# Thirteen pairs of up products a layer in place of twelve, and the block sums made kind by kind

## The chip, the cores and the metric

The kernel runs on one core of one Trainium2 chip. The time is the device time of one execution in microseconds (us); several runs are taken and their median is given. The core has five engines with queues of their own: TensorE (PE, matrix products), VectorE (DVE), ScalarE (ACT), GpSimd (POOL) and SyncE (SP, which issues the loads here). Products land in PSUM buffers, all else lies in SBUF.

## The reference

A trunk of two layers on x of 512 positions by 1024 features, float32. Each layer has a mixer (attention, a gated convolution and a recurrence, behind one input and one output projection), and then the part that matters here, a squared-ReLU MLP of 4096 hidden features:

```python
        x = x + mixed @ w_out[l]

        h = rms_norm(x, norm_mlp_g[l])
        x = x + jnp.square(jax.nn.relu(h @ w_mlp_up[l])) @ w_mlp_down[l]
    return rms_norm(x, final_norm_g)
```

## The kernel before

Everything is kept transposed: x is eight tiles `x[0..7]` of 128 features by 512 positions. Products are made nearly exact in float32 by splitting each operand into a rounded part (hi) and a rest (lo), and adding three products: hi·hi, hi·lo, lo·hi. So every weight block of 128x512 is loaded (`raw`, L339 or L1450), rounded by ScalarE (`whi`, L344; `shi_p`, L1455) and its rest taken by VectorE (`wlo`, L345; `slo_p`, L1456).

The MLP has 32 up groups of 128 hidden features. `up(i)` (L1405) makes one directly, a "single": 8 slices of the input, three matmuls of 512 columns each, 24 in all, through `mm3`. The first three singles are issued by TensorE within the end of the mixer. `two(i0, i1)` (L1443) makes two groups at once, a "pair": input, weights and output are cut in 2x2 blocks, and seven block products take the place of eight. A block product has 4 slices, three matmuls of 256 columns each; a pair has 7 × 12 = 84. Its seven products are p1, p5, p6, p2, p7, p3, p4 in that order, summed in three PSUM buffers `pa`, `pb`, `pc`. For them VectorE sums blocks of weights (`s1` to `s4`, L1461) and blocks of the input.

The sums of input blocks are the same for all pairs, and are made once a layer: `by_gain(j)` (L1420, ScalarE) writes `bn`, x with the norm's gain; `blocks(k)` (L1430) makes, for slice k, the four kinds of sums by VectorE subtractions of 128x256 (L1433 to L1436), ScalarE rounds them (`thi`), VectorE takes the rests (`tlo`, L1441). That is done for one k behind each of the singles 4 to 7.

Each up product goes through `square`: VectorE takes max(0, ·) times the norm's factor from PSUM (`r`, L1400), ScalarE squares it (`m`) and rounds it (`mh`), GpSimd takes the rest (`ml`, L1392). `mids` is the list of results, in ten buffers, and four of them make a "down group": `down(h, js)` (L1510) makes 8 tiles of 12 matmuls each, in two PSUM buffers in turn (tag "mm"), and VectorE adds each tile to x (`x<-dn`, L1516), which frees the buffer. The third tile waits for the first one's add.

The order in the MLP is: the singles; `down(0)`, all eight tiles; then the pairs, with half a down group (four tiles) behind a pair once `len(mids) >= 4 * h + 6`. With eight singles that holds after the first pair and after each one that follows, but for the last pairs of the last layer. Each engine runs its queue in order. That order is set at build time by a scheduler that places each instruction when it reckons its inputs and buffers to be there; so an instruction may stand earlier or later in its engine's queue than in the code.

`MID` (L184) is the order of the hidden features in mids, by which the host lays out the rows of the down weights.

Of the kernel before, what the change touches and what calls it, by code (L numbers as in the profile page):

```python
# [10 lines left out]
F32 = mybir.dt.float32  # L11
F32R = mybir.dt.float32r
# [4 lines left out]
ALU = mybir.AluOpType  # L17
# [6 lines left out]
P = 128  # L24
NK = D // P
# [150 lines left out]
         "wp/wlo 01201201201201202102102102102102102102102102102102102102102102102102102102 ")  # L176
NG = NG_IN + NG_OUT + NG_UP + NG_DN

N_ONE = 8

WHOLE = 5
PT = 1
N_TWO = (NG_UP - N_ONE) // 2
MID = tuple(range(N_ONE)) + tuple(N_ONE + i + N_TWO * j for i in range(N_TWO) for j in range(2))  # L184

# [83 lines left out]
def tile_trunk(ctx: ExitStack, tc: tile.TileContext, xT, wts, prm_d, cst_d, lora_d, gup_d, lam_d, fin_d, out):  # L269
    nc = tc.nc  # L270
    act, dve, pool = nc.scalar, nc.vector, nc.gpsimd
# [27 lines left out]
    def psum(tag, bufs, name):  # L299
        return ps.tile([P, 512], F32, tag=tag, bufs=bufs, name=name)  # L300
# [56 lines left out]
    def mm3(out_ps, w, acts, n=NK):  # L357
        for _ in mm3_steps(out_ps, w, acts, n):
            pass
# [12 lines left out]
    def norm_tile(j, key):  # L372

        if j == 0:
            acc = wp.tile([P, S], F32, tag="acc", bufs=1, name=f"acc{key}")
            nrm[key] = [acc]
            act.activation(acc, x[j], AF.Square)
        else:
            sq = wp.tile([P, S], F32, tag="sq", bufs=2, name=f"sq{key}_{j}")
            act.activation(sq, x[j], AF.Square)  # L380
            dve.tensor_tensor(nrm[key][0], nrm[key][0], sq, ALU.add)
# [187 lines left out]
    for l in range(L):  # L569
# [807 lines left out]
        with ExitStack() as mx:  # L1377
            fp = mx.enter_context(tc.tile_pool(name=f"fp{l}", bufs=1))
            spare[0] = fp
            RING = 10  # L1380
            H = S // 2
# [13 lines left out]
            def square(cs, name):  # L1395

                r = fp.tile([P, S], F32, tag="r", bufs=2, name=f"r{name}")
                for i, c in enumerate(cs):
                    q = slice(i * H, i * H + c.shape[1])
                    dve.scalar_tensor_tensor(r[:, q], c, 0.0, rs[:, q], ALU.max, ALU.mult)  # L1400
                m = fp.tile([P, S], F32, tag="m", bufs=3, name=f"m{name}")
                act.activation(m, r, AF.Square)
                kept(m)
# [9 lines left out]

            bn, th = {}, {}
            none = cp.tile([P, NB], F32, tag="rr", bufs=2, name=f"none{l}")[:, :1]
            dve.tensor_scalar(none, rs[:, :1], 0.0, None, ALU.is_lt)

            def by_gain(j):  # L1420

                if j == 0:
                    fp.tile([P, 8], F32, tag="pad0", name=f"pad0_{l}")
                bn[j] = fp.tile([P, 2, H], F32, tag="shi" if j < 4 else "slo", bufs=5, name=f"bn{l}_{j}")
                if j == 4:
                    fp.tile([P, 24], F32, tag="pad1", name=f"pad1_{l}")
                act.activation(bn[j].rearrange("p a s -> p (a s)"), x[j], AF.Identity, scale=pr[:, C_GMLP + j:C_GMLP + j + 1],
                               bias=none)

            def blocks(k):  # L1430
                b1, b2 = bn[k], bn[k + 4]
                t = [fp.tile([P, 2, H], F32, tag=f"s{2 * (k % 2) + i + 1}", name=f"t{l}_{k}_{i}") for i in range(2)]
                dve.tensor_tensor(t[0][:, 0], b1[:, 1], b1[:, 0], ALU.subtract)  # L1433
                dve.tensor_tensor(t[0][:, 1], b2[:, 1], t[0][:, 0], ALU.subtract)
                dve.tensor_tensor(t[1][:, 0], b2[:, 1], b1[:, 1], ALU.subtract)
                dve.tensor_tensor(t[1][:, 1], b2[:, 0], t[0][:, 1], ALU.subtract)  # L1436
                hi, lo = th[k] = [fp.tile([P, 4, H], F32R, tag=f"t{p}{k}", name=f"t{p}{l}_{k}") for p in ("hi", "lo")]
                for i in range(2):
                    u = slice(2 * i, 2 * i + 2)
                    act.copy(hi[:, u], t[i])  # L1440
                    dve.tensor_tensor(lo[:, u], t[i], hi[:, u].bitcast(F32), ALU.subtract)  # L1441

            def two(i0, i1):  # L1443

                n = f"{l}_{i0}"
                wg = wbase + NG_IN + NG_OUT

                def raw(i, a):
                    t = fp.tile([P, 4, P], F32, tag="sraw", bufs=6, name=f"raw{n}_{i}_{a}")
                    nc.sync.dma_start(t.rearrange("p k c -> p (k c)"), wts[wg + i, :, a * P:(a + 4) * P])  # L1450
                    return t

                def both(src, name):
                    hi, lo = [fp.tile([P, 4, P], F32R, tag=f"s{p}", bufs=5, name=f"s{p}{n}_{name}") for p in ("hi", "lo")]
                    act.copy(hi, src)  # L1455
                    dve.tensor_tensor(lo, src, hi.bitcast(F32), ALU.subtract)  # L1456
                    return hi, lo

                def sum_(name, a, b, op):
                    t = fp.tile([P, 4, P], F32, tag=name, name=f"{name}{n}")  # L1460
                    dve.tensor_tensor(t, a, b, op)  # L1461
                    return t

                def small(name):
                    return fp.tile([P, H], F32, tag=name, bufs=2, name=f"{name}{n}")

                def product(pt, w, moving, first=True):

                    whi, wlo = w
                    for k in range(4):  # L1470
                        ahi, alo = moving(k)
                        pe.matmul(pt, whi[:, k], ahi, start=(first and k == 0), stop=False, skip_group_check=True)
                        pe.matmul(pt, whi[:, k], alo, start=False, stop=False, skip_group_check=True)
                        pe.matmul(pt, wlo[:, k], ahi, start=False, stop=(k == 3), skip_group_check=True)

                blk = lambda d, q: lambda k: [p[:, q * H:(q + 1) * H] for p in acts[4 * d + k]]
                smm = lambda q: lambda k: [p[:, q] for p in th[k]]
                pa, pb = [psum("rp", 4, f"p{i}{n}")[:, :H] for i in "ab"]
                pc = psum("at", 2, f"pc{n}")[:, :H]
                c0 = fp.tile([P, S], F32, tag="c0", bufs=2, name=f"c0{n}")  # L1480
                w11 = raw(i0, 0)
                product(pa, both(w11, "p1"), blk(0, 0))
                p1 = small("p1")
                act.copy(p1, pa)
                w21 = raw(i1, 0)
                w22 = raw(i1, 4)
                s1 = sum_("s1", w21, w22, ALU.add)
                product(pb, both(s1, "p5"), smm(0))
                p5 = small("p5")
                dve.tensor_copy(p5, pb)  # L1490
                s2 = sum_("s2", s1, w11, ALU.subtract)
                product(pa, both(s2, "p6"), smm(1), False)
                u2 = small("u2")
                act.copy(u2, pa)
                w12 = raw(i0, 4)
                product(pc, both(w12, "p2"), blk(1, 0))
                dve.tensor_tensor(c0[:, :H], pc, p1, ALU.add)
                s3 = sum_("s3", w11, w21, ALU.subtract)
                product(pa, both(s3, "p7"), smm(2), False)
                c1 = small("c1")  # L1500
                act.copy(c1, pa)
                dve.tensor_tensor(c1, c1, p5, ALU.add)
                s4 = sum_("s4", w12, s2, ALU.subtract)
                product(pb, both(s4, "p3"), blk(1, 1), False)
                dve.tensor_tensor(c0[:, H:], pb, u2, ALU.add)
                square([c0], f"{n}_0")
                product(pa, both(w22, "p4"), smm(3), False)
                square([pa, c1], f"{n}_1")

            def down(h, js):  # L1510

                g, k0 = h // 2, 4 * (h % 2)
                for j in js:
                    pt = psum("mm", 2, f"dn{l}_{h}_{j}")
                    mm3(pt, weights(wbase + NG_IN + NG_OUT + NG_UP + 8 * g + j, k0, k0 + 4), mids[4 * h:4 * h + 4], 4)
                    dve.tensor_tensor(x[j], pt, x[j], ALU.add)  # L1516
                    if h == 2 * N_KG - 1 and j < NK - LATE:
                        norm_tile(j, f"m{l + 1}")


            for i in range(N_ONE):
                up(i)
                if i >= N_ONE - 4:
                    k = i - N_ONE + 4
                    by_gain(k)
                    by_gain(k + 4)
                    blocks(k)
            down(0, range(NK))
            h, half = 1, 0
            for p in range(N_TWO):  # L1530
                two(N_ONE + p, N_ONE + N_TWO + p)
                if len(mids) >= 4 * h + 6 and h < 2 * N_KG - 2 * (l == L - 1):
# [75 lines left out]
```

## Time and profile before

| | |
|---|---|
| runs | 1242.72, 1240.58, 1241.8 us; median 1241.8 |
| span of the profiled execution | 1241.5 us (no other time of it is given), granted clock 0.998 |
| busy: PE, DVE, ACT, POOL | 1230.0, 912.1, 675.0, 368.0 us |
| singles up_3 to up_7, layer 0 | 298.10 to 325.30 us |
| singles up_3 to up_7, layer 1 | 907.50 to 934.71 us |
| `down(0)`, layer 0 | 325.30 to 347.07 us |
| `down(0)`, layer 1 | 934.71 to 956.84 us |
| first pair, layer 0 | 347.07 to 357.07 us |
| last two pairs, layer 1 | 1166.11 to 1186.17 us |

Rows of the trace read: start, length (us), engine, line, operation, output<-inputs, shapes; in brackets the engine's idle time before it and what ended it. A row's length includes the time until its result is there, so that starts of neighbours (the pitch) tell what an engine spends on each. A row that is much longer than others of its shape was held up.

### The profile page before, as it was taken

How to read it: one execution, taken by the hardware profiler on the slowest of the kernel's cores; microseconds unless marked ns; L12 is line 12 of the kernel's file. 1: busy time of each engine (PE TensorE's matmuls, PEld its weight loads, DVE VectorE, ACT ScalarE, POOL GpSimd, SP SyncE). 2: the span in 40 equal slices, each digit the busy share in tenths (PEclk: the TensorE clock that was granted, in tenths of full speed). 3: DMA queues.
4: the chain of work that ended last, by engine and by line, in shares of the span. 5: the costliest groups of instructions: out<-in, count | busy, mean ns of one | idle time of the engine just before them, and what ended most of it. 6: DMA issues, size and time to landing. Idle time of an engine off the chain costs nothing.

```text
span 1241.5 us, 24974 instructions
## 1 busy us (share of the span) xinstructions
PE 1230.0 (99%) x9492; PEld 1055.0 (85%) x9492; DVE 912.1 (73%) x1776; ACT 675.0 (54%) x1410; POOL 368.0 (30%) x457
## 2 busy tenths in 40 slices
PE   9999999999999999999999999999999999999997
PEld 6888888888899998989887888888888999998987
DVE  6787888868767676765766777887687767676753
ACT  6785655548445454544464657464583445454542
POOL 1263637342311111111026355464231211111111
PEclk9999999999999999999999999999999999999999
DMA  6523324142433333321235244332433333333121
GB/s 216 163 87 99 105 96 111 53 153 85 136 102 98 107 94 106 99 85 44 69 106 164 79 118 119 89 83 73 158 102 120 102 102 98 107 94 107 55 68 68
DMA packets 84695, 127.90 MB, mean 103 GB/s; under 512 B 21472, under 2 KB 25568, under 8 KB 84576
## 3 DMA queue, kind: packets, MB, share of 16 engines
q1 hardware_dynamic: 83568, 125.64, 33.1%
q8 instruction: 74, 1.21, 0.4%
q10 hardware_dynamic: 1008, 0.68, 0.2%
q14 instruction: 45, 0.37, 0.1%
HBM read 117.11 MB, written 9.18 MB: 102 GB/s over the span
## 4 chain that ended last, share of the span: by engine, by line
PE 93%; ACT 2%; DVE 2%; DMA 1%; POOL 1%; issue 1%; ACTq 0%; POOLq 0%; DVEq 0%
PE dn L282 25%; PE pj L282 20%; PE pa L282 11%; PE po L282 8%; PE up L282 7%; PE pb L282 6%; PE dnF L282 4%; PE pc L282 3%; PE sc L282 1%; DMA raw<-wts 1%; PE ptt L287 1%; PE pg L282 1%; PE pyy L282 1%; PE pzw L282 1%; PE pst L282 1%
## 5 line engine op out<-in xcount | busy, mean ns | idle before, releaser
L1392 POOL TENSOR_TENSOR ml<-m,mh 128x512 fp32r<-128x512 f32 x64 | 108.9, 1716 | 481.0 <-ACT mh L1391 340.6
L344 ACT CAST whi<-raw 128x512 fp32r<-128x512 f32 x142 | 87.4, 619 | 162.4 <-PE dn L282 152.8
L282 PE MATMUL dn<-mh,whi 128*128 128x512 f32 x448 | 174.8, 390 | 0.1
L282 PE MATMUL dn<-ml,whi 128*128 128x512 f32 x448 | 174.6, 390 | 0.0
L282 PE MATMUL dn<-mh,wlo 128*128 128x512 f32 x448 | 174.5, 390 | 0.0
L683 POOL TENSOR_TENSOR wlo<-raw,whi 128x512 fp32r<-128x512 f32 x84 | 111.0, 1321 | 213.1 <-ACT whi L671 175.4
L282 PE MATMUL pj<-ahim,whi 128*128 128x512 f32 x392 | 156.7, 400 | 0.4 <-DVE vf L1278 0.4
L282 PE MATMUL pj<-ahim,wlo 128*128 128x512 f32 x392 | 156.4, 399 | 0.0
L282 PE MATMUL pj<-alom,whi 128*128 128x512 f32 x392 | 155.9, 398 | 0.0
L1516 DVE TENSOR_TENSOR x<-dn,x 128x512 f32<-128x512 f32 x112 | 77.3, 690 | 103.1 <-PE dn L282 103.1
L671 ACT CAST whi<-raw 128x512 fp32r<-128x512 f32 x142 | 87.6, 617 | 83.3 <-PE pj L282 25.1
L345 DVE TENSOR_TENSOR wlo<-raw,whi 128x512 fp32r<-128x512 f32 x142 | 115.0, 811 | 11.2 <-ACT whi L344 8.3
L282 PEld LDWEIGHTS dn<-mh,wlo 128*128 128x128 f32 x448 | 84.1, 188 | 17.8
L282 PEld LDWEIGHTS dn<-mh,whi 128*128 128x128 f32 x448 | 84.1, 188 | 17.5 <-issue 0.4
L282 PEld LDWEIGHTS dn<-ml,whi 128*128 128x128 f32 x448 | 84.1, 188 | 16.7
L1455 ACT CAST shi_p<-s 128x512 fp32r<-128x512 f32 x96 | 59.6, 621 | 70.1 <-PE pa L282 55.1
L282 PEld LDWEIGHTS pj<-ahim,whi 128*128 128x128 f32 x392 | 73.9, 188 | 14.1 <-issue 0.8
L282 PEld LDWEIGHTS pj<-alom,whi 128*128 128x128 f32 x392 | 73.9, 188 | 13.9 <-issue 0.5
L282 PEld LDWEIGHTS pj<-ahim,wlo 128*128 128x128 f32 x392 | 73.9, 188 | 13.8 <-issue 0.2
L1456 DVE TENSOR_TENSOR slo_p<-s,shi_p 128x512 fp32r<-128x512 f32 x96 | 67.9, 708 | 19.7 <-ACT shi_p L1455 17.2
L282 PE MATMUL pa<-tlo,shi_p 128*128 128x256 f32 x288 | 81.3, 282 | 0.0
L282 PE MATMUL pa<-thi,shi_p 128*128 128x256 f32 x288 | 81.2, 282 | 0.0
(414 smaller groups left out, 3208.1 us busy)
## 6 DMA issues: line engine op xcount, KB each, us to landing
raw<-wts SPq DMA_DIRECT2D x389, 256.0 KB, 2.7
qs<-dqhi SPq DMA_DIRECT2D x24, 128.0 KB, 3.7
ks<-dkhi SPq DMA_DIRECT2D x24, 128.0 KB, 3.7
x<-xT SPq DMA_DIRECT2D x8, 256.0 KB, 4.6
dqhi<-qhi SPq DMA_DIRECT2D x6, 256.0 KB, 3.4
dqlo<-qlo SPq DMA_DIRECT2D x6, 256.0 KB, 3.4
dkhi<-khi SPq DMA_DIRECT2D x6, 256.0 KB, 2.7
dklo<-klo SPq DMA_DIRECT2D x6, 256.0 KB, 3.5
```

Of the source, the lines that this page charges most:

```text
L282: ins = nc.tensor.matmul(*a, **k)
L287: ins = nc.tensor.transpose(*a, **k)
L344: act.copy(hi[:, :n], raw[:, :n])
L345: (pool if a and lean[0] else dve).tensor_tensor(lo[:, :n], raw[:, :n], hi[:, :n].bitcast(F32), ALU.subtract)
L671: yield act.copy(hi[:, k0:k1], raw[:, k0:k1])
L683: yield eng.tensor_tensor(lo[:, k0:k1], raw[:, k0:k1], hi[:, k0:k1].bitcast(F32), ALU.subtract)
L1392: pool.tensor_tensor(lo, m, hi.bitcast(F32), ALU.subtract)
L1455: act.copy(hi, src)
L1456: dve.tensor_tensor(lo, src, hi.bitcast(F32), ALU.subtract)
L1516: dve.tensor_tensor(x[j], pt, x[j], ALU.add)
```

## The change

`N_ONE` goes from 8 to 6: six singles and thirteen pairs a layer. `by_gain` of all eight tiles stands behind the singles and ahead of `down(0)`; `blocks` stands behind `down(0)` in the code and makes one kind q of sum for all slices, where it made all four kinds for one slice. The sums are written to the tiles `s3`, `s4` and `c0`, where they took `s1` to `s4`. The subtractions, casts and rests are as many as before, of the same shapes. `down(0)` stood ahead of the pairs before too; with six singles the condition for a half down holds only after the second pair, so that pairs one and two follow each other directly. A layer has two weight blocks of 128x512 (whi, wlo) less per single that goes, and one pair more of weight sums.

```diff
-N_ONE = 8
+N_ONE = 6
...
-            def blocks(k):
-                b1, b2 = bn[k], bn[k + 4]
-                t = [fp.tile([P, 2, H], F32, tag=f"s{2 * (k % 2) + i + 1}", name=f"t{l}_{k}_{i}") for i in range(2)]
-                dve.tensor_tensor(t[0][:, 0], b1[:, 1], b1[:, 0], ALU.subtract)
-                dve.tensor_tensor(t[0][:, 1], b2[:, 1], t[0][:, 0], ALU.subtract)
-                dve.tensor_tensor(t[1][:, 0], b2[:, 1], b1[:, 1], ALU.subtract)
-                dve.tensor_tensor(t[1][:, 1], b2[:, 0], t[0][:, 1], ALU.subtract)
-                hi, lo = th[k] = [fp.tile([P, 4, H], F32R, tag=f"t{p}{k}", name=f"t{p}{l}_{k}") for p in ("hi", "lo")]
+            def blocks(q):
+                hi, lo = th[q] = [fp.tile([P, 4, H], F32R, tag=f"t{p}{q}", name=f"t{p}{l}_{q}") for p in ("hi", "lo")]
                 for i in range(2):
                     u = slice(2 * i, 2 * i + 2)
-                    act.copy(hi[:, u], t[i])
-                    dve.tensor_tensor(lo[:, u], t[i], hi[:, u].bitcast(F32), ALU.subtract)
+                    t = fp.tile([P, 2, H], F32, tag="c0" if q == 1 else ("s3", "s4")[i], bufs=1 + (q == 1), name=f"t{l}_{q}_{i}")
+                    for k in (2 * i, 2 * i + 1):
+                        b1, b2, o = bn[k], bn[k + 4], t[:, k % 2]
+                        if q == 0:
+                            dve.tensor_tensor(o, b1[:, 1], b1[:, 0], ALU.subtract)
+                        elif q == 1:
+                            dve.tensor_tensor(o, b2[:, 1], tb[0, i][:, k % 2], ALU.subtract)
+                        elif q == 2:
+                            dve.tensor_tensor(o, b2[:, 1], b1[:, 1], ALU.subtract)
+                        else:
+                            dve.tensor_tensor(o, b2[:, 0], tb[1, i][:, k % 2], ALU.subtract)
+                    tb[q, i] = t
+                    act.copy(hi[:, u], t)
+                    dve.tensor_tensor(lo[:, u], t, hi[:, u].bitcast(F32), ALU.subtract)
...
-                smm = lambda q: lambda k: [p[:, q] for p in th[k]]
+                smm = lambda q: lambda k: [p[:, k] for p in th[q]]
...
             for i in range(N_ONE):
                 up(i)
-                if i >= N_ONE - 4:
-                    k = i - N_ONE + 4
-                    by_gain(k)
-                    by_gain(k + 4)
-                    blocks(k)
+            for j in range(NK):
+                by_gain(j)
             down(0, range(NK))
+            for q in range(4):
+                blocks(q)
```

Three places in the engines' queues show what the scheduler made of it. In all names the digit in front is the layer, the last number a buffer's.

The first is VectorE in layer 1, from the last single's r to the adds of the first tiles of `down(0)`. Before:

```order
L1400 SCALAR_TENSOR_TENSOR r1_7_11973<-up1_7_11936,rsf1_11639 128x512
L345 TENSOR_TENSOR wlo167_0_12061<-raw167_0_12058,whi167_0_12060 128x512
L1516 TENSOR_TENSOR x0_69<-dn1_0_0_11997,x0_69 128x512
L345 TENSOR_TENSOR wlo168_0_12081<-raw168_0_12078,whi168_0_12080 128x512
L1516 TENSOR_TENSOR x1_70<-dn1_0_1_12017,x1_70 128x512
L345 TENSOR_TENSOR wlo169_0_12101<-raw169_0_12098,whi169_0_12100 128x512
L1516 TENSOR_TENSOR x2_71<-dn1_0_2_12037,x2_71 128x512
```

The same place with the change:

```order
L1400 SCALAR_TENSOR_TENSOR r1_5_11903<-up1_5_11866,rsf1_11709 128x512
L345 TENSOR_TENSOR wlo167_0_11993<-raw167_0_11990,whi167_0_11992 128x512
L1447 TENSOR_TENSOR tlo1_3_12126<-t1_3_1_12132,thi1_3_12125 128x512
L1462 TENSOR_TENSOR slo1_6_p5_12168<-s11_6_12165,shi1_6_p5_12167 128x512
L1462 TENSOR_TENSOR slo1_6_p6_12188<-s21_6_12185,shi1_6_p6_12187 128x512
L1522 TENSOR_TENSOR x0_69<-dn1_0_0_11929,x0_69 128x512
L345 TENSOR_TENSOR wlo168_0_12013<-raw168_0_12010,whi168_0_12012 128x512
L1462 TENSOR_TENSOR slo1_6_p2_12208<-raw1_6_6_4_12205,shi1_6_p2_12207 128x512
L1467 TENSOR_TENSOR s31_6_12224<-raw1_6_6_0_12141,raw1_6_19_0_12161 128x512
L1522 TENSOR_TENSOR x1_70<-dn1_0_1_11949,x1_70 128x512
```

Rests of block sums and the first pair's weight work now stand between the last single's r and the first add (x0), and between the adds. From up_3's r up to that add there are 26 instructions, 18 of 128x512 and 8 of 128x256, in layer 1 and in layer 0.

The second is TensorE in layer 1 within the second pair, which now follows the first one directly. With the change:

```order
L282 MATMUL pb1_7_12298<-thi1_0_12089,slo1_7_p5_12328 128x256
L282 MATMUL pc1_7_12299<-ahif1_4_11631,shi1_7_p2_12367 128x256
L282 MATMUL pc1_7_12299<-alof1_4_11632,shi1_7_p2_12367 128x256
L282 MATMUL pc1_7_12299<-ahif1_4_11631,slo1_7_p2_12368 128x256
L282 MATMUL pc1_7_12299<-ahif1_5_11642,shi1_7_p2_12367 128x256
L282 MATMUL pc1_7_12299<-alof1_5_11643,shi1_7_p2_12367 128x256
L282 MATMUL pa1_7_12297<-thi1_1_12101,shi1_7_p6_12347 128x256
L282 MATMUL pa1_7_12297<-tlo1_1_12102,shi1_7_p6_12347 128x256
```

Five matmuls of p2 (pc) stand ahead of p6 (pa, thi1_1); in every other pair, before and after, p5, p6 and p2 follow each other whole. Layer 0's second pair has the same order.

The third is VectorE at the end of the mixer of layer 0, a piece of the difference:

```order
 L753 TENSOR_TENSOR accf0_3856<-accf0_3856,sqf0_1_3874 128x512
+L1467 TENSOR_TENSOR s10_6_4565<-raw0_6_19_0_4561,raw0_6_19_4_4563 128x512
 L724 TENSOR_TENSOR x2_71<-po0_2_4_3868,x2_71 128x512
 L740 SCALAR_TENSOR_TENSOR alof0_1_3881<-x1_70,prm0_66,ahif0_1_3880 128x512
+L1467 TENSOR_TENSOR s20_6_4585<-s10_6_4565,raw0_6_6_0_4541 128x512
 L724 TENSOR_TENSOR x3_72<-po0_3_4_3895,x3_72 128x512
 L753 TENSOR_TENSOR accf0_3856<-accf0_3856,sqf0_3_3925 128x512
```

The first pair's sums s1 and s2 now stand between the adds of the mixer's output to x (x<-po); in layer 1 they stand between the adds of x2 and x3.

More of the change, by code (lines that the diff above doesn't have):

```diff
@@ L1412, in up @@
                 square([pt], f"{l}_{i}")
-            bn, th = {}, {}
+            bn, th, tb = {}, {}, {}
             none = cp.tile([P, NB], F32, tag="rr", bufs=2, name=f"none{l}")[:, :1]
```

## The prediction

> **What bounds the kernel now.** I read the page first, then TensorE (PE) through the four stretches of the MLP that the change touches, then what VectorE (DVE) did there.
>
> The page's first and fourth parts say which engine sets the end.
>
> ```profile
> PE 1230.0 (99%) x9492; PEld 1055.0 (85%) x9492; DVE 912.1 (73%) x1776; ACT 675.0 (54%) x1410; POOL 368.0 (30%) x457
> PE 93%; ACT 2%; DVE 2%; DMA 1%; POOL 1%; issue 1%; ACTq 0%; POOLq 0%; DVEq 0%
> ```
>
> TensorE is busy 99% of the span and holds 93% of the chain that ended last. So the change pays by matmul time removed, and costs by every gap it opens between matmuls. The busy times by stretch show who could open one; columns are the stretch, its length, the busy time of PE, its weight loads, DVE, ACT and POOL with counts, the granted clock, DMA share and GB/s. The first two rows are singles of layer 0, then come down(0), a pair, a half down, and the singles of layer 1 from up_3 on.
>
> ```profile
> 298.10:308.98 10.88, 10.88 (x50) 9.01 (x48) 10.85 (x22) 9.56 (x17) 2.15 (x2) 1.00 0.24 74
> 308.98:325.30 16.32, 16.32 (x74) 13.51 (x72) 16.27 (x24) 9.70 (x18) 9.20 (x3) 1.00 0.50 150
> 325.30:347.07 21.77, 21.77 (x98) 18.02 (x96) 12.19 (x17) 6.82 (x13) 2.58 (x2) 1.00 0.37 119
> 347.07:357.07 10.00, 10.00 (x86) 10.00 (x84) 8.09 (x15) 5.12 (x10) 0.00 (x0) 1.00 0.31 102
> 357.07:367.99 10.92, 10.92 (x50) 9.01 (x49) 7.34 (x12) 4.72 (x9) 3.39 (x2) 1.00 0.35 100
> 907.50:934.70 27.20, 27.20 (x121) 22.52 (x120) 27.06 (x46) 19.99 (x35) 9.65 (x4) 1.00 0.36 112
> ```
>
> During the singles VectorE is as full as TensorE (10.85 of 10.88, 16.27 of 16.32, 27.06 of 27.20 us). It gets air only in down(0): 12.19 of 21.77. A pair takes 8.09 of 10.00. The clock was 1.00 throughout.
>
> **The matmuls.** The starts of two singles, of a pair and of the half down after it:
>
> ```profile
> 303.54 0.39 PE L282 MATMUL up<-ahif,whi 128*128 128x512 f32 x1
> 314.42 0.39 PE L282 MATMUL up<-ahif,whi 128*128 128x512 f32 x1
> 347.07 0.28 PE L282 MATMUL pa<-ahif,shi_p 128*128 128x256 f32 x1
> 357.07 0.40 PE L282 MATMUL dn<-mh,whi 128*128 128x512 f32 x1
> ```
>
> Two singles are 48 matmuls in 314.42 − 303.54 = 10.88 us, 0.2267 each. A pair is 84 matmuls of 256 columns in 357.07 − 347.07 = 10.00 us, 0.119 each. One pair in place of two singles saves 0.88 a layer: **−1.76 us** in two layers. The Trainium skill ("TensorE: Matmul & The Clock Gate", section "Wait — 56ns, not 53.3ns?") gives a warm matmul N ÷ 2.4 GHz plus about 2.5 ns; as an estimate from that page the two singles would be 10.36 us, the pair 9.17, and the saving 2.4 us in all. The rows pay 12 to 13 ns over N ÷ 2.4 GHz per matmul, not 2.5, and a pair has 36 more of them; here the measurement decides.
>
> **down(0) starts a pair's time sooner, where VectorE is behind.** Its tiles share two PSUM buffers, so the third tile (dn_0_2) waits until VectorE's add of the first (x<-dn, L1516) is done. Layer 1 already pays for that:
>
> ```profile
> 934.71 0.39 PE L282 MATMUL dn<-mh,whi 128*128 128x512 f32 x1
> 939.54 0.68 DVE L1516 TENSOR_TENSOR x<-dn,x 128x512 f32<-128x512 f32 x1
> 939.92 0.39 PE L282 MATMUL dn<-mh,wlo 128*128 128x512 f32 x1
> 940.36 0.47 PE L282 MATMUL dn<-mh,whi 128*128 128x512 f32 x1
> 940.67 0.40 PE L282 MATMUL dn<-ml,whi 128*128 128x512 f32 x1
> ```
>
> The add ended at 940.22, the third tile began at 940.36, 0.14 later. From 939.92 two steps took 0.44 and 0.31 instead of 0.227: 0.30 us lost. In layer 0 the add began at 328.56 and cost nothing:
>
> ```profile
> 328.56 0.68 DVE L1516 TENSOR_TENSOR x<-dn,x 128x512 f32<-128x512 f32 x1
> ```
>
> Now down(0) starts where up_6 started, and the third tile, 24 matmuls or 5.44 us later, is due where up_7 started, at 929.26 in layer 1:
>
> ```profile
> 912.95 0.39 PE L282 MATMUL up<-ahif,whi 128*128 128x512 f32 x1
> 923.83 0.39 PE L282 MATMUL up<-ahif,whi 128*128 128x512 f32 x1
> 929.26 0.39 PE L282 MATMUL up<-ahif,whi 128*128 128x512 f32 x1
> ```
>
> In VectorE's new order 26 instructions stand from up_3's r up to that add, in both layers: 18 of 512 columns and 8 of 256 (block sums made kind by kind, four tlo or more, casts' rests, the r of up_4 and up_5, the first pair's slo). All of them are now queued ahead of the add that frees the buffer. Their pitch comes from uninterrupted neighbours:
>
> ```profile
> 933.03 0.68 DVE L1461 TENSOR_TENSOR s<-raw,s 128x512 f32<-128x512 f32 x1
> 933.63 0.68 DVE L1461 TENSOR_TENSOR s<-raw,raw 128x512 f32<-128x512 f32 x1
> 916.54 0.41 DVE L1434 TENSOR_TENSOR t<-bn,t 128x256 f32<-128x256 f32 x1
> 916.87 0.41 DVE L1435 TENSOR_TENSOR t<-bn,bn 128x256 f32<-128x256 f32 x1
> ```
>
> That is 0.60 and 0.34. So 18 × 0.60 + 8 × 0.34 = 13.5 us, then the add's 0.68 and the 0.14: 14.3. up_3's matmuls end at 912.95; a matmul's row is 0.39 long at a pitch of 0.23, so its last result comes 0.16 later, and 16.15 us are left until 929.26. It would fit with 1.8 to spare, but for two things. First, GpSimd's ml (L1392) and VectorE hold each other up:
>
> ```profile
> 912.12 1.53 POOL L1392 TENSOR_TENSOR ml<-m,mh 128x512 fp32r<-128x512 f32 x1 [5.86 <-ACT mh L1391]
> 912.60 1.61 DVE L345 TENSOR_TENSOR wlo<-raw,whi 128x512 fp32r<-128x512 f32 x1
> 918.03 1.75 POOL L1392 TENSOR_TENSOR ml<-m,mh 128x512 fp32r<-128x512 f32 x1 [4.37 <-ACT mh L1391]
> 927.81 1.19 DVE L345 TENSOR_TENSOR wlo<-raw,whi 128x512 fp32r<-128x512 f32 x1
> 930.73 1.78 DVE L1456 TENSOR_TENSOR slo_p<-s,shi_p 128x512 fp32r<-128x512 f32 x1
> ```
>
> One VectorE instruction per ml is stretched, from 0.68 to 1.19, 1.61 or 1.78: +0.5 to +1.1, about 0.9. The ml of up_3 and up_4 fall in the stretch for certain, that of up_5 at its end: 1.8 to 2.7 us. The Trainium skill ("SBUF — State Buffer", section "Who interferes with whom") says that a DVE instruction with two SBUF inputs and a GpSimd one that reads SBUF exclude each other for a whole instruction, and that one with at most one SBUF input does not contend. The trace agrees so far as it goes: the stretched ones, 1.61 and 1.78, have two SBUF inputs. It speaks against this change, since nearly all of the 26 are of that kind.
>
> Second, r itself may be late. Before, up_3's r began 2.39 us after up_3 ended:
>
> ```profile
> 915.34 0.68 DVE L1400 SCALAR_TENSOR_TENSOR r<-up,rsf 128x512 f32<-128x512 f32 x1
> ```
>
> The new order has less ahead of it: from up_2's r on 4 full and 4 half instructions (3.8 us) in layer 1 and 6 and 2 (4.3) in layer 0, against a single's 5.44. So I bound its lateness by 0 and 1 us.
>
> Need: 14.3 + 1.8 = 16.1 to 14.3 + 2.7 + 1 = 18.0, against 16.15: a gap of **0 to 1.9 us in each layer**. The nearest rows, the same add in the kernel before, gave 0 and 0.30 after singles in which VectorE was as full. The middle is 0.95; those rows pull it down, and I take 0.7 a layer, **+1.4 us**. The 0.30 of before goes away with its place: **−0.30**. The later adds are 4 or 5 instructions apart (2.4 to 3.0 us) against a tile's 12 × 0.2267 = 2.72, so the loss is not repeated. mids 0 to 3 are ready in time: up_3's ml ended at 919.78 before (the row at 918.03), and is wanted from 923.83 on.
>
> **Two pairs back to back.** No half down stands between pairs one and two now, so VectorE's 8.09 a pair, plus what a half down used to absorb, meets 10.00 us of matmuls. In the second pair the new order puts five matmuls of p2 ahead of p6, so p2's rest (slo) is wanted sooner. It is the 14th instruction after the add of down(0)'s last tile, which can't begin before the first pair does. At 0.60 and 0.34, with the waits for the first pair's p2 (5.72 us from its start) and p3 (8.57) between them, it is done some 9.8 us after the first pair began, and p2 wants it at 10.00 + 26 × 0.119 = 13.1. The lead of about 3 us also covers a raw block that lands at the 5.6 us of the row further down instead of 2.7. The last two pairs of layer 1 already run so, and the dearest step there was this:
>
> ```profile
> 1178.96 0.35 PE L282 MATMUL pa<-thi,shi_p 128*128 128x256 f32 x1
> 1179.15 0.28 PE L282 MATMUL pa<-tlo,shi_p 128*128 128x256 f32 x1
> ```
>
> 0.19 instead of 0.119. I take 0.1 a layer, **+0.2**, between 0 and 0.35 a layer, five such steps. ScalarE gets six more instructions a layer; at 5.12 of 10.00 a pair they hide.
>
> **The first pair's two sums** move to the end of the mixer in each layer (their tiles no longer hold block sums): 2 × 0.60 a layer on VectorE, between the adds x<-po. Those adds wait for TensorE, not it for them:
>
> ```profile
> 268.83 0.69 DVE L724 TENSOR_TENSOR x<-po,x 128x512 f32<-128x512 f32 x1 [0.36 <-PE po L282]
> 274.27 0.69 DVE L724 TENSOR_TENSOR x<-po,x 128x512 f32<-128x512 f32 x1 [1.43 <-PE po L282]
> DMA to landing us min/median/max: 2.5/2.7/5.6
> ```
>
> An add may be some 0.6 late and has a tile's 2.72 before its buffer is wanted; two adds on, the idle 1.43 swallows it. The sums also wait for their raw weights, issued at the places of before and landed 2.5 to 5.6 us later. Cost: 0, at most 0.3; with the cover gone, 4 × 0.60 = 2.4. Two fewer rests of weights and one r a layer are gone, and the block sums are as many as before; they are in the count above.
>
> **The sum**: −1.76 − 0.30 + 1.4 + 0.2 = −0.46. On the profiled span, 1241.5, that is 1241.0. The median of the runs, 1241.8, lies 0.3 above the span, so the forecast is **1241.3 us**. Bounds: −2.06 with no gap at all (1239.7), −2.06 + 3.8 + 0.7 + 0.3 = +2.74 with all of them (1244.5). The three runs spread over 2.1 us, so I call 0.2%, 2.5 us, what can be told from no change.
>
> **Rivals.**
>
> *The gain arrives whole.* The two ml that must fall in the stretch go into gaps, r is on time, and the third tile finds its buffer free: −2.06, **1239.7**. For it: 0.05 us to spare at the lower end, and layer 0 lost nothing before. Against it: layer 1's add began at 939.54, 1.9 us after its tile's end (934.71 + 2.72 + 0.16).
>
> *The queue on VectorE decides.* All three ml hit, and r is 1 us late, in both layers: the third tile of each down(0) waits 1.9 us; from about 1.0 a layer (2.06 in all) on the change loses. −2.06 + 3.8 = +1.7, **1243.5**; with the other costs at their ends too, 1244.5. For it: VectorE had 27.06 of 27.20 us busy where now 10.9 us less come before the add. Against it: two singles' r, m and rests are gone from that stretch.
>
> *The pairs don't run at 10.00.* The second pair's new order, or block sums that come late for p5, open gaps in each of the two. The pair's saving is gone at 0.88 a layer: −0.30 + 1.4 = +1.1, **1242.9**. Against it: every pair of before took 10.00, and the last tlo stands ahead of the add in the order, over 15 us before p5.
>
> **How the numbers follow.** Likeliest, part of the gain eaten (1240.3 to 1242.5): 0.45. The whole gain, down to 1239.4 with the runs' spread: 0.22. The queue decides, 1242.5 to 1245: 0.25. Pairs not at 10.00 or anything else: 0.08. The range 1239.4 to 1244.2 leaves out about 2 in 10. Faster by over 2.5 us needs less than 1239.3, more than the whole sum: 0.10, from the whole gain with a saving at the page's size or a lucky median. Slower by over 2.5 needs more than 1244.3: 0.14, about half of the queue's case and some of the last. Within: 0.76.
>
> **What would show it.** 13 pairs of 10.00 us a layer. dn_0_2 begins 5.44 after dn_0_0 if the gain is whole, 6.1 if I am right, 7.3 if the queue decides; the row to read is x<-dn of the first tile and how many stretched rows stand ahead of it. Between pair one and pair two no step over 0.2 us. The forecast is wrong if gaps open elsewhere: at the end of the mixer by the early sums, at p5 of the first pair by late block sums, or in the first half of down(1), whose mids now come straight from the first pair.

## The result

The changed kernel takes 1245.06 us (median of 13 runs, 1244.07 to 1245.84), the kernel before 1242.81 in 13 runs, the three of the forecast among them: a ratio of 1.0020, 95% interval 1.0013 to 1.0027. That is 2.25 us slower, where 0.5 us faster was forecast; 1245.06 lies above the range's end of 1244.2. The median of the 13 runs of before lies 1.0 us above that of the three on which the forecast stood, so some 2.7 us of the miss is the change's and 1.0 the base's.

The busy times by engine from the profile's page of the changed kernel, and then those of three stretches of its layer 0: the singles up_4 and up_5, `down(0)`, and the first two pairs (columns as in the prediction). Where a fence has three dots, rows between are left out.

```profile
PE 1231.1 (99%) x9564; PEld 1057.3 (85%) x9564; DVE 923.9 (74%) x1800; ACT 680.0 (55%) x1422; POOL 366.1 (29%) x457
```

```profile
304.50:315.41 10.91, 10.91 (x50) 9.01 (x48) 10.91 (x19) 8.73 (x16) 6.12 (x2) 1.00 0.32 94
315.41:338.76 23.35, 22.47 (x98) 17.79 (x97) 17.88 (x30) 7.22 (x13) 2.08 (x1) 1.00 0.44 137
338.76:359.27 20.51, 20.44 (x169) 20.11 (x168) 17.37 (x29) 12.20 (x24) 2.96 (x2) 1.00 0.33 103
```

TensorE is as busy as before, but `down(0)` takes 23.35 us where its matmuls need 21.77, and the first two pairs take 20.51 where they need 20.00. VectorE has 17.88 us of work in `down(0)`, before 12.19.

Stage by stage, from the starts of the matmuls in the two traces:

| stage | before | after | difference |
|---|---|---|---|
| up to the first up matmul of layer 0 | 279.51 | 280.47 | +0.96 |
| singles, layers 0 and 1 | 45.79, 46.23 | 34.94, 35.35 | −21.73 |
| `down(0)` | 21.77, 22.13 | 23.35, 22.81 | +1.58, +0.68 |
| first pair; first two pairs | 10.00, 10.00 | 20.52, 20.49 | +21.01 |
| the other pairs and half downs, to the layer's end or the last group | 262.87, 219.33 | 263.14, 219.73 | +0.27, +0.40 |
| mixer of layer 1 | 268.54 | 267.51 | −1.03 |
| last group | 49.39 | 49.40 | +0.01 |

TensorE spends each stage on matmuls and on waits between them; a wait is told here as what a step from one matmul's start to the next takes over the pitch. The MLP stages, rows two to five, went from 638.13 to 640.32 us in sum: +2.19. The first row and the mixer differ from profile to profile whatever the kernel: over all twelve profiles of this study the first was 278.57 to 281.02, the mixer 267.35 to 268.54. (In before's mixer of layer 1 a raw weight block landed 5.50 us after its issue, and TensorE lost 1.2 us by it that it did not lose there in the changed kernel.) So kernels are compared below by the sum of the MLP stages, and by their times.

**The third tile of `down(0)`.** TensorE, then VectorE from up_3's r on, then GpSimd, all in the changed kernel's layer 0.

```profile
320.62 0.39 PE L282 MATMUL dn<-mh,wlo 128*128 128x512 f32 x1
321.87 0.47 PE L282 MATMUL dn<-mh,whi 128*128 128x512 f32 x1 [0.86 <-ACT shi_p L1461]
```

```profile
305.92 0.68 DVE L1400 SCALAR_TENSOR_TENSOR r<-up,rsf 128x512 f32<-128x512 f32 x1
...
312.15 1.19 DVE L345 TENSOR_TENSOR wlo<-raw,whi 128x512 fp32r<-128x512 f32 x1
313.26 2.38 DVE L1447 TENSOR_TENSOR tlo<-t,thi 128x512 fp32r<-128x512 f32 x2
...
321.04 0.68 DVE L1522 TENSOR_TENSOR x<-dn,x 128x512 f32<-128x512 f32 x1
321.64 1.17 DVE L345 TENSOR_TENSOR wlo<-raw,whi 128x512 fp32r<-128x512 f32 x1
```

```profile
302.35 1.29 POOL L1392 TENSOR_TENSOR ml<-m,mh 128x512 fp32r<-128x512 f32 x1 [3.78 <-ACT mh L1391]
308.06 4.72 POOL L1392 TENSOR_TENSOR ml<-m,mh 128x512 fp32r<-128x512 f32 x1 [4.42 <-ACT mh L1391]
313.69 1.40 POOL L1392 TENSOR_TENSOR ml<-m,mh 128x512 fp32r<-128x512 f32 x1 [0.90 <-ACT mh L1391]
320.17 2.08 POOL L1392 TENSOR_TENSOR ml<-m,mh 128x512 fp32r<-128x512 f32 x1 [5.09 <-ACT mh L1391]
```

The add began at 321.04, ended at 321.72, and the tile at 321.87: 1.25 us after the matmul ahead of it, 1.02 more than the pitch. The releaser that the row names is inferred and does not fit; the add's end does, as in the kernel before, 0.15 ahead. In layer 1 the same step took 0.93, 0.70 more than the pitch. Two ml after r (308.06 and 313.69) fall ahead of the add and lengthen VectorE's work there by 0.5 (312.15) and 1.1 us (2.38 for two where 1.28 is usual); the third one hits just behind it (321.64), so that the next two tiles wait 0.13 and 0.26 more.

**The second pair** waits for ScalarE. TensorE: the last matmul of p1, the last one of p2 that the order put ahead, and p6's first. Then ScalarE:

```profile
350.06 0.28 PE L282 MATMUL pa<-ahif,slo_p 128*128 128x256 f32 x1
...
352.08 0.28 PE L282 MATMUL pc<-alof,shi_p 128*128 128x256 f32 x1
352.43 0.39 PE L282 MATMUL pa<-thi,shi_p 128*128 128x256 f32 x1
```

```profile
349.93 0.63 ACT L1402 ACTIVATE m<-r 128x512 f32<-128x512 f32 x1 [0.46 <-DVE r L1400]
350.46 0.60 ACT L1461 CAST shi_p<-s 128x512 fp32r<-128x512 f32 x1
350.97 0.62 ACT L1391 CAST mh<-m 128x512 fp32r<-128x512 f32 x1
351.49 0.63 ACT L1402 ACTIVATE m<-r 128x512 f32<-128x512 f32 x1
352.03 0.35 ACT L1490 COPY p<-pa 128x256 f32<-128x256 f32 x1
```

p6 adds onto p1 in the same PSUM buffer, so p1 must be copied out first. p1 was done at 350.34, its copy ran from 352.03 to 352.38, behind the squares and casts of the first pair's results. p6 began at 352.43.

**The first half of `down(1)`** waits 0.25 us in layer 0 and 0.36 in layer 1 at its third tile: VectorE's add is late again. Ahead of it, in layer 0, VectorE stood idle until a raw weight block landed; in layer 1 it was idle for 1.35 us ahead of the same sum, and the trace names no releaser. TensorE and VectorE in layer 0:

```profile
364.53 0.39 PE L282 MATMUL dn<-mh,wlo 128*128 128x512 f32 x1
364.89 0.50 PE L282 MATMUL dn<-mh,whi 128*128 128x512 f32 x1
```

```profile
351.71 1.79 DVE L1467 TENSOR_TENSOR s<-raw,raw 128x512 f32<-128x512 f32 x1
...
353.76 1.45 DVE L1467 TENSOR_TENSOR s<-raw,s 128x512 f32<-128x512 f32 x1
...
358.60 0.69 DVE L1467 TENSOR_TENSOR s<-raw,raw 128x512 f32<-128x512 f32 x1 [1.25 <-DMA raw<-wts]
364.15 0.69 DVE L1522 TENSOR_TENSOR x<-dn,x 128x512 f32<-128x512 f32 x1
```

The sums at 351.71 and 353.76 are 1.9 us longer in all than the usual 0.69, while GpSimd makes the first pair's two ml (351.67 to 354.66). No run here separates these ml from the load as the cause of the wait.

**The early sums** made an add late too, at the end of layer 0's mixer. VectorE, GpSimd and TensorE:

```profile
267.50 1.22 DVE L1467 TENSOR_TENSOR s<-raw,raw 128x512 f32<-128x512 f32 x1 [1.36 <-DMA raw<-wts]
268.65 0.68 DVE L724 TENSOR_TENSOR x<-po,x 128x512 f32<-128x512 f32 x1
```

```profile
266.88 1.29 POOL L683 TENSOR_TENSOR wlo<-raw,whi 128x512 fp32r<-128x512 f32 x1 [12.77 <-ACT whi L671]
```

```profile
268.66 0.39 PE L282 MATMUL po<-mhi,wlo 128*128 128x512 f32 x1
269.47 0.47 PE L282 MATMUL po<-mhi,whi 128*128 128x512 f32 x1 [0.42 <-DVE x L724]
```

The sum s1 waited 1.36 us for its weights and then took 1.22 where 0.69 is usual, beside a GpSimd subtraction that had begun 0.62 ahead of it; the add behind it ended at 269.33, and TensorE lost 0.66 us (0.81 and 0.31 where 0.227 each is the pitch). In layer 1, where the sum waited 1.01 us and took 0.69, it lost 0.08.

The wait for the weights alone does not make the 0.66. In five of the kernels below (blocks_only, no_ml, p1_dve, six_p1, split_six) GpSimd began ahead of the sum as well; the sum waited 0.93 to 1.35 us and took 1.24 to 1.67, and the loss was 0.66 each time. In six_buf the weights came before GpSimd began, at 266.10, and TensorE lost nothing:

```profile
265.64 0.69 DVE L1467 TENSOR_TENSOR s<-raw,raw 128x512 f32<-128x512 f32 x1 [0.30 <-DMA raw<-wts]
```

### The profile page after: what moved, and what is told of

Same layout as the page of the kernel before. It is cut to its first block, busy times and chain, and to the rows that moved or that the text cites. A ratio compares the mean times of both kernels' runs of the same rounds, so it can differ in the third digit from the quotient of the medians.

```text
span 1243.6 us, 25171 instructions
## 1 busy us (share of the span) xinstructions
PE 1231.1 (99%) x9564; PEld 1057.3 (85%) x9564; DVE 923.9 (74%) x1800; ACT 680.0 (55%) x1422; POOL 366.1 (29%) x457
## 4 chain that ended last, share of the span: by engine, by line
PE 90%; DVE 4%; ACT 2%; issue 1%; DMA 1%; POOL 0%; ACTq 0%; POOLq 0%; SPq 0%; DVEq 0%
PE dn L282 24%; PE pj L282 21%; PE pa L282 11%; PE po L282 8%; PE pb L282 6%; PE up L282 4%; PE dnF L282 4%; PE pc L282 3%; PE sc L282 1%; DMA raw<-wts 1%; PE ptt L287 1%; PE pg L282 1%; PE pyy L282 1%; DVE slo_p L1462 1%; PE pzw L282 1%
## 5 line engine op out<-in xcount | busy, mean ns | idle before, releaser
L344 ACT CAST whi<-raw 128x512 fp32r<-128x512 f32 x134 | 82.9, 619 | 159.2 <-PE dn L282 149.6
L671 ACT CAST whi<-raw 128x512 fp32r<-128x512 f32 x142 | 87.6, 617 | 77.1 <-PE pj L282 26.3
L345 DVE TENSOR_TENSOR wlo<-raw,whi 128x512 fp32r<-128x512 f32 x134 | 110.0, 821 | 10.5 <-ACT whi L344 8.7
L1461 ACT CAST shi_p<-s 128x512 fp32r<-128x512 f32 x104 | 64.4, 621 | 73.4 <-PE pa L282 59.0
L282 PE MATMUL pa<-thi,shi_p 128*128 128x256 f32 x312 | 88.4, 283 | 0.1
L282 PE MATMUL pa<-tlo,shi_p 128*128 128x256 f32 x312 | 88.1, 282 | 0.0
L282 PE MATMUL pa<-thi,slo_p 128*128 128x256 f32 x312 | 87.4, 280 | 0.0
L1462 DVE TENSOR_TENSOR slo_p<-s,shi_p 128x512 fp32r<-128x512 f32 x104 | 72.3, 697 | 19.7 <-ACT shi_p L1461 17.2
```

The source lines that it names most:

```text
L282: ins = nc.tensor.matmul(*a, **k)
L344: act.copy(hi[:, :n], raw[:, :n])
L345: (pool if a and lean[0] else dve).tensor_tensor(lo[:, :n], raw[:, :n], hi[:, :n].bitcast(F32), ALU.subtract)
L671: yield act.copy(hi[:, k0:k1], raw[:, k0:k1])
```

## The experiments

"MLP" is the sum of the MLP stages in the profile; before 638.13, after 640.32. It leaves out what the early sums cost in the mixer. Each time is the median of 10 or 11 runs, of 4 for pairs_only and 5 for late_sums, and stands beside runs of the kernel before on the same chip, 1242.49 to 1242.63 us. Between two variants the intervals often overlap, as for p1_dve or late_sums and the changed kernel (1.0013 to 1.0027); then only MLP, of one profile each, tells them apart. In a stage that was left alone it repeats within 0.2 us: the ten kernels with six singles took 34.86 to 35.05 us for those of layer 0, and 35.30 to 35.48 in layer 1.

| kernel | time | ratio to before, 95% | MLP |
|---|---|---|---|
| blocks_only | 1242.45 | 1.0002 (0.9993 to 1.0011) | 637.79 |
| pairs_only | 1253.62 | 1.0086 (1.0072 to 1.0100) | 648.10 |
| six_buf | 1242.12 | 0.9997 (0.9988 to 1.0006) | 637.94 |
| no_ml | 1242.75 | 1.0003 (0.9994 to 1.0012) | 637.52 |
| p1_dve | 1244.03 | 1.0013 (1.0004 to 1.0021) | 639.29 |
| six_p1 | 1242.67 | 1.0002 (0.9993 to 1.0011) | 637.86 |
| split | 1243.44 | 1.0011 (1.0002 to 1.0020) | 639.11 |
| late_sums | 1245.90 | 1.0032 (1.0019 to 1.0044) | 642.02 |
| split_six | 1241.28 | 0.9989 (0.9981 to 0.9998) | 636.08 |
| all3 | 1240.32 | 0.9981 (0.9972 to 0.9990) | 636.13 |

### The change's two halves

`blocks_only`, in the changed kernel:

```diff
-N_ONE = 6
+N_ONE = 8
```

`pairs_only`, in the kernel before:

```diff
-N_ONE = 8
+N_ONE = 6
```

> The change's block order alone: eight singles and twelve pairs as before, block sums made kind by kind in s3, s4 and c0. The first theory, from the gaps between matmuls in the changed kernel's trace: the early sums s1 and s2 cost 0.66 us at the end of layer 0's mixer and 0.19 in layer 1's, and nothing else in the block order costs; so the kernel before plus 0.5 to 1.0 us, with one gap of some 0.6 at an output-projection product in layer 0. The rival, that the order by kind makes VectorE late: the third tile of down(0) waits 1 us or more in each layer, plus 2 us.

> Thirteen pairs and six singles with the block sums as in the kernel before (all four kinds for one slice, behind each of the singles 2 to 5). The first theory: the waits come from the number of singles, not from the order of the block sums; down(0)'s third tile waits 0.7 to 1.5 us in each layer, the second pair loses 0.4 to 0.5, there are no early sums; slower than the kernel before by 1 to 2 us. The rival, that the block order by kind is what made VectorE late: no wait over 0.3 us at down(0), and 1 to 2 us faster than before.

The block order alone makes no difference that can be told. Its MLP is 0.34 us shorter than before's: the 0.30 at layer 1's third tile is gone. It has the early sums' gap, 0.66 us in layer 0, as the first theory said; the 0.5 to 1.0 us that it forecast for the time do not show.

The thirteenth pair alone is 11 us slower, far more than either theory gave. Both of its `down(0)` wait at the third tile, 2.2 and 2.9 us over the pitch. So the block order by kind was not what made VectorE late; with six singles it relieved it (`down(0)` takes 25.03 and 26.54 us here, 23.35 and 22.81 with it). In layer 1 the wait was long enough for something else; three stretches from the last matmul ahead of it on:

```profile
931.80:935.00 3.20, 0.48 (x3) 0.06 (x1) 3.20 (x5) 1.46 (x4) 1.60 (x1) 0.98 0.26 82
935.00:938.50 3.50, 3.44 (x9) 2.75 (x10) 3.50 (x7) 0.48 (x1) 0.00 (x0) 0.53 0.79 250
938.50:945.00 6.50, 6.50 (x30) 5.27 (x29) 3.71 (x7) 1.32 (x3) 0.00 (x0) 1.00 0.52 159
```

After a gap of 3.17 us from start to start the granted clock was 0.53 for the next 3.5 us. The four runs go from 1251.46 us, the profiled one, with a mean granted clock of 0.997, to 1255.12 with 0.994, so part of their spread goes with the clock. Besides, its half downs take 11.00 to 11.04 us each in place of 10.93, in both layers, spread over all their matmuls and not as a wait; the cause stays open.

### The third tile's wait

`six_buf`:

```diff
-                    pt = psum("mm", 2, f"dn{l}_{h}_{j}")
+                    pt = psum("rp", 4, f"dn{l}_{h}_{j}") if h == 0 and j % 4 > 1 else psum("mm", 2, f"dn{l}_{h}_{j}")
```

`no_ml`:

```diff
-                pool.tensor_tensor(lo, m, hi.bitcast(F32), ALU.subtract)
+                if 3 <= i < N_ONE:
+                    pool.memset(lo.bitcast(F32), 0.0)
+                else:
+                    pool.tensor_tensor(lo, m, hi.bitcast(F32), ALU.subtract)
```

> The changed kernel, with two of every four tiles of down(0) in the four PSUM buffers that the singles used, so that six buffers serve it in place of two. The first theory: the late add x<-dn of the first tile is what holds TensorE, 1.49 us in layer 0 and 0.99 in layer 1; with a buffer free the gaps go, 2.2 to 2.5 us less than the changed kernel. The rival: VectorE is behind as a whole, and the wait only moves to the first pair's weights; less than 0.7 us is gained.

> The changed kernel, where GpSimd writes zeros in place of the rests ml of the singles 3, 4 and 5 in each layer: those three rests are left out of the down products, and GpSimd reads nothing there. If it is GpSimd's ml that stretches one VectorE instruction each by about 0.9 us, VectorE's queue ahead of the first add is 1.8 to 2.7 us shorter, the third tile of down(0) waits 0.2 us at most and the kernel is 1.5 to 2.3 us faster than the changed one. If the number of instructions alone makes the add late, the wait stays at 0.8 to 1.1 us in each layer and nothing is gained.

With the buffers `down(0)` takes 21.77 us in both layers, and 2.4 us of MLP are gained: the wait did not move to the first pair. So what TensorE waited for was the PSUM buffer that the late add holds.

Without the three ml, whose part the down products then lack, it takes 21.77 too, with two buffers and the same instructions on VectorE:

```profile
306.47 0.68 DVE L1403 SCALAR_TENSOR_TENSOR r<-up,rsf 128x512 f32<-128x512 f32 x1
...
313.29 1.28 DVE L1450 TENSOR_TENSOR tlo<-t,thi 128x512 fp32r<-128x512 f32 x2
...
319.98 0.67 DVE L1525 TENSOR_TENSOR x<-dn,x 128x512 f32<-128x512 f32 x1
```

From r to the add are 13.51 us, where 18 × 0.60 + 8 × 0.34 is 13.52; in the changed kernel they are 15.12. In layer 1 they are 13.53 and 15.11. So two ml cost VectorE 1.6 us, and without these 1.6 us there is no wait.

### The second pair and `down(1)`

`p1_dve` (and `six_p1`, with the edit of `six_buf` beside it):

```diff
-                act.copy(p1, pa)
+                dve.tensor_copy(p1, pa)
```

`split`:

```diff
-            down(0, range(NK))
+            down(0, range(4))
...
                 two(N_ONE + p, N_ONE + N_TWO + p)
+                if p == 0:
+                    down(0, range(4, NK))
```

> The changed kernel with the copy of p1 out of PSUM on VectorE in place of ScalarE, in all pairs. The first theory: in the second pair p6 waits for that copy, which stands on ScalarE behind the squares and casts (m, mh) of the first pair's two results; on VectorE it is not behind them, the second pair runs at 10.0 us and the kernel is 0.8 to 1.0 us faster than the changed one. The rival: VectorE is what is late in the second pair, and 26 copies more of 0.34 us make it worse; not faster, or slower.

> The changed kernel with down(0) cut in two halves, four tiles ahead of the first pair and four behind it, so that no two pairs follow each other at the start. The first theory: the gaps within the second pair (0.52 and 0.49 us) and in the first half of down(1) (0.25 and 0.36) come from two pairs in a row and go; the third tile's wait stays; 1.3 to 1.7 us less than the changed kernel. The rival: the first pair now comes 10.9 us sooner, VectorE has not made its weights and block sums by then, and gaps in the first pair take back 1 us or more.

> The changed kernel with six PSUM buffers for down(0) and p1's copy on VectorE, the pairs still back to back. If the two waits are separate, their gains add: the buffers gave 2.6 us and the copy 0.7 less than the changed kernel, so 3.2 less, about 1 us under the kernel before (1241.5), with only the first half of down(1) still waiting. If VectorE's extra copies take back what the buffers gave, it is no faster than the version with the buffers alone.

With p1's copy on VectorE both pairs take 20.00 us in both layers, and five matmuls of p2 no longer stand ahead of p6 in the order; 1.0 us of MLP is gained. So it was the copy's place on ScalarE; the order of the matmuls came of it, since the edit touches only the copy.

With the buffers as well, the gains do not add: MLP is 637.86, against 637.94 without the copy's edit. The pairs are at 20.00, but the first half of `down(1)` now waits 0.51 us in layer 0 and 1.37 in layer 1, where it waited 0.29 and 0.71:

```profile
964.82 0.69 DVE L1467 TENSOR_TENSOR s<-raw,raw 128x512 f32<-128x512 f32 x1 [1.63 <-DMA raw<-wts]
970.38 0.68 DVE L1522 TENSOR_TENSOR x<-dn,x 128x512 f32<-128x512 f32 x1
```

```profile
969.63 0.39 PE L282 MATMUL dn<-mh,wlo 128*128 128x512 f32 x1
971.11 0.50 PE L282 MATMUL dn<-mh,whi 128*128 128x512 f32 x1 [1.10 <-DVE x L1522]
```

TensorE arrives sooner, VectorE's add at 970.38 does not (970.23 without the edit): a wait ahead of a later one pays only as far as the later one lets it. VectorE stood idle for a raw weight block there. The waits of SyncE's queue in the changed kernel, from 336 to 362 us (who is waited for: us, times, longest), show what such a load waits for:

```profile
SPq L1456 <- DVE slo_p L1462: 14.1, 5, 4.4
SPq L339 <- DVE wlo L345: 4.6, 2, 2.3
```

The loads wait for VectorE to have read their buffers, and VectorE then for the loads. Which of the two is first stays open.

`split` ends both: no gap in the second pair, and `down(1)` runs at its pitch in both layers. The third tile's wait stays, as expected, and in layer 1 the second half of `down(0)` waits 0.66 us at its third tile, which was not expected. The gain is 1.21 us of MLP, less than the 1.3 to 1.7 expected.

### The early sums, and a version that beats both

`late_sums`:

```diff
-                    t = fp.tile([P, 2, H], F32, tag="c0" if q == 1 else ("s3", "s4")[i], bufs=1 + (q == 1), name=f"t{l}_{q}_{i}")
+                    t = fp.tile([P, 2, H], F32, tag="c0" if q == 1 else f"s{i + (1 if q == 0 else 3)}", bufs=1 + (q == 1), name=f"t{l}_{q}_{i}")
```

`all3` has the edits of `split`, `six_buf` and `late_sums`, `split_six` those of `split` and `six_buf`.

> The changed kernel with the block sums written to s1, s2 (first kind), c0 (second) and s3, s4 (third and fourth), so that the first pair's sums s1 to s4 cannot be made before the block sums are. The first theory: no VectorE instruction waits for a raw weight block in the mixer, the gap of up to 0.66 us in layer 0 and 0.19 in layer 1 goes; the sums now stand in the full stretch, where the queue ahead of down(0)'s first add is as long as in the changed kernel in layer 0 and half a us longer in layer 1; in all 0 to 0.8 us less than the changed kernel. The rival: the early sums relieved VectorE in the full stretch, and without them the third tile waits longer by 1 us or more; slower than the changed kernel.

> The changed kernel with three edits: down(0) cut in halves around the first pair, two of every four of its tiles in the singles' PSUM buffers, and the block sums in s1 to s4 so that no sum is early. The first theory: each wait that was found has its edit, none moves, and the saving of 1.76 us and the 0.30 of before arrive; 1.7 to 2.1 us less than the kernel before, a ratio of 0.9983 to 0.9986. The rival: with the first pair 10.9 us sooner VectorE lacks the air that the second half of down(0) gave it, and gaps of 1 us and more open in the first pair; no faster than the kernel before.

> The faster version (halves around the first pair, singles' PSUM buffers) without the third of its edits: the block sums in s3, s4 and c0 as in the changed kernel, so that the first pair's sums are early again. With the change's sums moved to the full stretch the kernel had been 0.85 us slower, so the early sums help VectorE there; but with more PSUM buffers a late add costs nothing. If the early sums' wait for their raw weights in the mixer is what is left, this is 0.2 to 0.7 us slower than the version with all three edits, 1240.5 to 1241; if relief in the full stretch counts here too, it is equal or up to 0.5 us faster.

Without early sums the gap in the mixer is gone, but MLP is 1.7 us longer, and the kernel is not faster than the changed one: the rival held in the main. The third tile's step is 1.4 and 1.9 us over the pitch, where it was 1.02 and 0.70, and `down(0)` takes 0.70 and 1.20 us more. In layer 1:

```profile
929.89 0.39 PE L282 MATMUL dn<-mh,wlo 128*128 128x512 f32 x1
932.05 0.47 PE L282 MATMUL dn<-mh,whi 128*128 128x512 f32 x1 [1.77 <-DVE x L1522]
```

Three of the first pair's sums, 0.60 us each, now stood ahead of that add in the full stretch, where the changed kernel has one in layer 0 and none in layer 1.

Where a late add costs nothing, this turns round. With all three edits no step from `down(0)` to the last pair is a tenth of a us over its pitch, in both layers, and MLP takes 636.13 us: 2.00 less than before, within 0.06 the 1.76 and the 0.30 of the prediction's sum. The time is 1240.32, 2.3 us under the kernel before, and by the two ratios 4.8 under the changed one. Its first add comes 6.01 us after `down(0)` begins, later than the 5.63 of the changed kernel, while TensorE goes on:

```profile
319.78 0.39 PE L282 MATMUL dn<-mh,wlo 128*128 128x512 f32 x1
320.00 0.39 PE L282 MATMUL dn<-mh,whi 128*128 128x512 f32 x1
```

```profile
320.57 0.68 DVE L1522 TENSOR_TENSOR x<-dn,x 128x512 f32<-128x512 f32 x1
```

With early sums left in, MLP is the same (636.08) and the mixer has its 0.66 us gap again; the time is 1.0 us longer, but the two intervals overlap.

## Why the prediction was wrong

The saving came, but four costs were set too low: `down(0)` cost 2.62 us where 1.4 was taken, the two pairs back to back 1.01 where 0.2 was, and the first half of `down(1)`, 0.67, and the early sums, 0.74, stood at nothing. On the base of the three runs, 1241.8, the changed kernel would have come out at 1244.05, inside the range; that would have been luck, since it would have been slower all the same.

- **Pairs for singles, −1.76**: right. Singles −21.73, the pairs' matmuls +20.00, so −1.73; every other pair took 10.00. The pitch of the rows held, and with it this saving, not the 2.4 us that the smaller pitch would have given.
- **The 0.30 of before**: 0.36 by the stage.
- **`down(0)`, 0 to 1.9 a layer, 0.7 taken**: the mechanism was right, in place and in price; the size taken was too small. Over the 21.77 of its matmuls it lost 1.58 and 1.04, 2.62 in all against +1.4. The third tile began 6.46 and 6.14 us after the first, 1.02 and 0.70 late, so that 0.3 of the miss lies there. Within it, 13.5 us for the 26 instructions was exact. The ml took 1.6, less than the 1.8 to 2.7 of the estimate, since the third one hit behind the add. But r was 1.2 us late in layer 0 and 0.9 in layer 1, where the bound was 1 us. The other 0.9 came of "the loss is not repeated", which was wrong: the third ml stretched VectorE's work between the adds, and later tiles waited (0.39 in layer 0, 0.13 in layer 1; the rest in steps of under 0.1).
- **Two pairs back to back, +0.2, at most 0.7**: this step failed. The pairs lost 1.01. I counted VectorE's instructions up to p2, and they were in time; but the five matmuls ahead of p6 stood there for ScalarE, whose copy of p1 has to wait for the first pair's squares and casts; with the copy elsewhere the pairs lost nothing. "At 5.12 of 10.00 a pair they hide" took a share of busy time for an answer about one instruction's place in a queue.
- **`down(1)`**: no price was set; it was only named as what would make the forecast wrong. It lost 0.67. What a half down between pairs gave VectorE was noted, and not carried to the next add; what makes that add late is not settled.
- **The early sums, 0, at most 0.3**: 0.66 and 0.08. The idle 0.36 and 1.43 belong to the adds of x3 and x5, but s1 stands ahead of the add of x2: it waited for its weights at the head of VectorE's queue, and with it the add, and in layer 0 it fell beside a GpSimd subtraction and was stretched. "The sums also wait for their raw weights" stood there without a price, and the hold-up by GpSimd was priced at `down(0)` alone. Where the weights came before GpSimd began, nothing was lost (six_buf).
- **The sum**: −1.73 − 0.36 + 2.62 + 1.01 + 0.67 + 0.74 = +2.95 in the profile, where −0.46 was forecast. The spans differ by 2.1, since before's mixer of layer 1 was the longest of the twelve; the times differ by 2.25.
- **The rivals**: the queue on VectorE does decide more than half of it, but no rival held all the waits together; adding the ends of all costs gave +2.74, which came nearest.

## What to carry to other kernels

Work pulled forward on the bound engine makes the helpers' deadlines sooner: count, for each place where the bound engine reuses a buffer, what is queued on the helper ahead of the instruction that frees it, on every helper, with the loads it waits for. A share of busy time does not answer that. Where a freeing instruction is late but its data is not wanted, another buffer takes the whole wait away (2.4 us here); where several waits follow each other, removing one may gain nothing, since the next one takes it up (moving p1's copy gained 1.0 us by itself, 0.1 with the buffers).

## What the hardware showed

A GpSimd subtraction and VectorE's two-input ones hold each other up: an ml takes 1.29 to 1.30 us at its shortest, up to 4.72 against a full VectorE, and cost it 0.5 to 1.1 us each. The Trainium skill ("SBUF — State Buffer", section "Who interferes with whom") has a VectorE instruction with two SBUF inputs contend with a GpSimd one that reads SBUF; the trace agrees, and `no_ml` shows the price, 1.6 us for two. By the rows, a late ml got in at a VectorE instruction that reads PSUM. Around `down(0)`'s start four ml of the changed kernel took over 2 us: those at 308.06 and 320.17 in layer 0, and in layer 1 those at 918.01 (3.64 us) and 929.72 (2.08). They ended 1.21 to 1.24 us after an r (311.55, 920.41) or the first add itself (321.04, 930.58) began, and the row behind that one is the stretched one. So the third ml fell behind the add in both layers.

TensorE's clock fell after one wait: after a gap of 3.17 us in the thirteenth-pair-only kernel the granted clock was 0.53 and the matmuls' pitch 0.427 us for some 3 us, while a gap of 2.43 us in the same kernel's layer 0 was followed by the full pitch. The Trainium skill ("TensorE: Matmul & The Clock Gate", section "What's actually happening") has the clock halved after an idle window of about 3.4 us; the trace agrees in the halving, but here a gap shorter than that was enough.
